# One MLP's second product as seven block products instead of eight, with operands that pass through DRAM

## The chip, the core and the metric

The kernel runs on one core of a Trainium2 chip. The core has five engines, each with its own queue of instructions that it works through in order: TensorE (PE) multiplies matrices and writes to PSUM, VectorE (DVE) and ScalarE (ACT) do elementwise work, GpSimd (POOL) does elementwise work on SBUF alone, and SyncE (SP) issues the DMA transfers between DRAM and SBUF. The engines meet at semaphores. The metric is the time of one execution on the device in microseconds (us); the number given for a kernel is the median of several runs.

## The reference, cut to what matters

The reference is one inference step of a decoder with two layers, for a prompt of 1024 positions and 32 sample positions (1056 columns in all). Layer 0 mixes dilated attention and causal pooling, layer 1 is an mLSTM block, and after each of them stands a squared-ReLU MLP with a residual:

```
def sq_relu_ffn(x, w1, w2):
    h = jax.nn.relu(x @ w1)
    return (h * h) @ w2
...
        hp = hp + sq_relu_ffn(rms_norm(hp, norm_ffn[layer]), ffn_w1[layer], ffn_w2[layer])
```

with x of width 1024, w1 of 1024x4096 and w2 of 4096x1024. The change is in the MLP of layer 0 alone.

## The kernel before, in words

Activations lie transposed: 128 channels on the partitions, the 1056 positions along the free dimension. A product is made to high precision from three passes. Each operand is split into a rounded part and a rest (`split`, L97: the rounded part by ACT at L106, the rest by a DVE or POOL subtraction at L107), and `mm3` (L129) multiplies rounded by rounded, rounded by rest and rest by rounded into one PSUM bank. The columns come in three pieces, `CH`: 384, 384 and 288.

`ffn` (L236) works through the 4096 hidden channels in eight blocks of 512. For a block it makes four rows of 128 hidden channels (first product: eight k tiles, three passes, three column pieces, so 72 matmuls a row). DVE takes a finished bank out with relu and the norm's factor (L254), ACT squares it (L255) and rounds it (L106), DVE makes the rest (L107). Then `project_into` (L262) multiplies the block by its part of w2 (second product: eight output rows of 128, four k tiles, three passes, three pieces) and DVE adds each bank to the residual `x` (L274). The weights of a row or a pair of rows are one DMA of 512 KB into `wraw` and a split by ACT and POOL.

In the last block every finished piece of `x` is also fed onward (`feed`, L181): two DVE instructions scale it by the next norm's gain and split it into the operands `xg` of the next layer (L187 and L188), ACT squares it (L199), POOL sums the squares (L201), and `finish_norm` turns the sum into the factor `R`. The next layer's first product, `project(0)` in `up_project`, reads `xg`, and its banks are multiplied by `R`.

A framework schedules the program: it keeps the order of each engine's queue by priorities and its own estimates, gives out buffers as they come free, and sets the semaphore waits. A pool that is opened where another was closed takes its memory, and waits for that memory's last readers and writers. In the MLP of layer 0 there are four PSUM banks (`self.psum(4)`).

Of the kernel before, what the change touches and what calls it, by code (L numbers as in the profile page):

```python
# [22 lines left out]
CH = [(0, 384), (384, 384), (768, 288)]  # L23
FF = 4096
FB = 512
EPS = 1e-6

H, HD = 8, 64
# [15 lines left out]
def weave(*steps, beat=lambda: None):  # L44

    order = sorted(((k + 0.5) / n, i) for i, (_, n) in enumerate(steps) for k in range(n))
    for _, i in order:
        next(steps[i][0], None)
        beat()


def late(n, gen):

    for _ in range(n):
        yield
    yield from gen
# [11 lines left out]
class Net:  # L68
# [4 lines left out]
    def __init__(self, tc, a):  # L73
        self.tc, self.nc, self.a = tc, tc.nc, a
        nc = self.nc
        self.cms = []
        self.consts = self.pool("consts")
        self.wpool = self.pool("wpool", bufs=2)
        self.gains = self.consts.tile([P, 5, KD], F32, name="gains")
        self.ident = self.consts.tile([P, P], F32, name="ident")  # L80
        self.ones = self.consts.tile([P, P], F32, name="ones")
        nc.gpsimd.memset(self.ones, 1.0)
        self.mhalf = self.consts.tile([P, 16], F32, name="mhalf")
        nc.gpsimd.memset(self.mhalf, -0.5)
# [3 lines left out]
        self.due, self.parts = [], {}  # L88
        self.beside, self.pace = None, 0

    def pool(self, name, bufs=1, side="left", **kw):
# [34 lines left out]
            self.split(w[0][:, k], w[1][:, k], raw[:, k], eng=eng)  # L126
        return w

    def mm3(self, ps, w, x, first=True, last=True):  # L129

        mm = self.nc.tensor.matmul
        mm(ps, w[0], x[0], start=first, stop=False)  # L132
        mm(ps, w[0], x[1], start=False, stop=False)  # L133
        mm(ps, w[1], x[0], start=False, stop=last)  # L134

    def psum(self, bufs):
        self.pmm, self.tag, self.bufs = self.pool("pmm", space=PSUM), "mm", bufs
# [97 lines left out]
    def ffn(self, layer, x, xg, fed, beside=None):  # L235

        nc = self.nc
# [20 lines left out]
        if layer:  # L258
            self.settle()
        self.close(hp)  # L260

    def project_into(self, x, unit, xs, fed=None, first=None, pool=None):  # L262

# [464 lines left out]
    def up_project(self, keep):  # L728
# [23 lines left out]
        def project(m):  # L752
# [84 lines left out]
        rest = (None for m in range(16) for _ in outer(m))  # L837
        left = 15
        for m in range(16):
            weave((project(m), 13), *([(late(3, follow(*self.made)), 11)] if m else []))  # L840
# [741 lines left out]
```

## Time and profile before

| | |
|---|---|
| median of 3 runs | 3201.49 us (3197.26 to 3202.69) |
| the profiled execution | 3198.09 us, span of its trace 3196.3 us |
| PE busy | 3100.5 us, 97% of the span, 19702 matmuls |
| DVE busy | 1675.6 us, 52% |
| ACT busy | 995.4 us, 31% |
| POOL busy | 923.2 us, 29% |
| the MLP of layer 0 | from 548 us to 1300 us of the span |
| granted TensorE clock, mean | 0.992 of full speed |

Times in the trace count from the start of the span. Busy time of PE is the time in which at least one matmul is under way; matmuls are pipelined, so the time that one matmul adds is read from the distance between two starts, not from its own duration. A wait is put down to the semaphore that came last.

### The profile page before, as it was taken

The numbers are of one execution on the slowest core, as the hardware profiler recorded it, in microseconds if no ns is written. First come the engines' busy times: TensorE is split into PE (matmuls) and PEld (weight loads), VectorE is DVE, ScalarE is ACT, GpSimd is POOL, SyncE is SP. The second block draws the span as 40 slices with busy tenths as digits, with TensorE's granted clock in tenths as the row PEclk, the third lists the DMA queues.
The fourth block names the chain that finished last, engine by engine and source line by source line (L and its number), as shares of the span: only waits on it lengthen the run. The fifth ranks groups of instructions, "written<-read, shape, count | busy, mean of one in ns | idle before, by whom it ended". The sixth has DMA issues, their size and how long they took to land.

```text
span 3196.3 us, 48197 instructions
## 1 busy us (share of the span) xinstructions
PE 3100.5 (97%) x19702; PEld 2888.7 (90%) x19702; DVE 1675.6 (52%) x3139; ACT 995.4 (31%) x1828; POOL 923.2 (29%) x691
## 2 busy tenths in 40 slices
PE   7999999999999999999998999998999999999998
PEld 7775578999999999999998888878999999999998
DVE  7765537333333335666565477766365444444434
ACT  4443212222211123222223565654123222222222
POOL 4110014221122223434333354543142212121223
PEclk9999999999999999999999999999999999999999
DMA  4113561111111111333323466555314444444411
GB/s 134 45 47 131 179 228 40 42 45 47 47 47 47 47 47 67 103 107 110 102 94 122 146 207 222 179 165 179 107 40 137 150 159 165 148 155 142 146 60 68
DMA packets 198790, 355.85 MB, mean 111 GB/s; under 512 B 25540, under 2 KB 103108, under 8 KB 195752
## 3 DMA queue, kind: packets, MB, share of 16 engines
q1 hardware_dynamic: 198568, 352.77, 32.7%
q8 instruction: 154, 2.52, 0.3%
q14 instruction: 68, 0.56, 0.1%
HBM read 263.61 MB, written 89.11 MB: 110 GB/s over the span
## 4 chain that ended last, share of the span: by engine, by line
PE 81%; DVE 10%; POOL 2%; ACT 2%; issue 2%; DMA 2%; SPq 0%; DVEq 0%; POOLq 0%; ACTq 0%
PE mm L132 23%; PE mm L134 22%; PE mm L133 22%; PE po L406 1%; PE nq L132 1%; PE mm L534 1%; DVE xg L188 1%; PE nq L134 1%; PE nq L133 1%; PE pt L390 1%; PE pc L1320 1%; DVE x L274 1%; DVE xg L187 1%; PE acc L1263 1%; POOL xm L107 1%
## 5 line engine op out<-in xcount | busy, mean ns | idle before, releaser
L107 POOL TENSOR_TENSOR w<-wraw,w 128x1024 fp32r<-128x1024 f32 x196 | 478.2, 2440 | 1524.9 <-ACT w L106 1513.5
L132 PE MATMUL mm<-xg,w 128*128 128x384 f32 (+1 forms) x2664 | 886.6, 333 | 15.0 <-ACT xg L458 6.7
L134 PE MATMUL mm<-xg,w 128*128 128x384 f32 (+1 forms) x2664 | 866.0, 325 | 7.6 <-POOL w L107 7.6
L133 PE MATMUL mm<-xg,w 128*128 128x384 f32 (+1 forms) x2664 | 866.2, 325 | 4.3 <-DVE xg L459 4.3
L132 PEld LDWEIGHTS mm<-xg,w 128*128 128x128 f32 x2664 | 504.3, 189 | 59.6 <-issue 43.9
L274 DVE TENSOR_TENSOR x<-mm,x 128x384 f32<-128x384 f32 (+1 forms) x528 | 275.3, 523 | 531.4 <-PE mm L134 523.0
L133 PEld LDWEIGHTS mm<-xg,w 128*128 128x128 f32 x2664 | 505.0, 190 | 13.0 <-DVE xg L459 5.8
L134 PEld LDWEIGHTS mm<-xg,w 128*128 128x128 f32 x2664 | 503.8, 189 | 12.2 <-POOL w L107 9.2
L132 PE MATMUL mm<-h,w 128*128 128x384 f32 (+1 forms) x1536 | 497.5, 324 | 0.0
L134 PE MATMUL mm<-h,w 128*128 128x384 f32 (+1 forms) x1536 | 497.1, 324 | 0.0
L133 PE MATMUL mm<-h,w 128*128 128x384 f32 (+1 forms) x1536 | 495.9, 323 | 0.0
L106 ACT ACTIVATE w<-wraw 128x1024 fp32r<-128x1024 f32 (+1 forms) x202 | 210.7, 1046 | 807.5 <-PE mm L133 643.5
L107 DVE TENSOR_TENSOR h<-hr,h 128x384 fp32r<-128x384 f32 (+1 forms) x192 | 198.8, 1035 | 213.6 <-ACT h L106 213.6
L133 PEld LDWEIGHTS mm<-h,w 128*128 128x128 f32 x1536 | 289.1, 188 | 3.6
L134 PEld LDWEIGHTS mm<-h,w 128*128 128x128 f32 x1536 | 288.8, 188 | 0.0
L132 PEld LDWEIGHTS mm<-h,w 128*128 128x128 f32 x1536 | 288.7, 188 | 0.0
L254 DVE SCALAR_TENSOR_TENSOR hr<-mm,rstd 128x384 f32<-128x384 f32 (+1 forms) x192 | 100.6, 524 | 259.5 <-PE mm L134 259.4
L255 ACT ACTIVATE hr<-hr 128x384 f32<-128x384 f32 (+1 forms) x192 | 94.6, 493 | 382.8 <-DVE hr L254 382.7
L779 DVE SCALAR_TENSOR_TENSOR ca<-ext,chan,ca 128x1080 f32<-128x1080 f32 x48 | 132.8, 2766 | 1.5
L132 PE MATMUL mm<-yh,w 128*128 128x384 f32 (+1 forms) x384 | 126.0, 328 | 6.0 <-ACT yh L106 6.0
L133 PE MATMUL mm<-yh,w 128*128 128x384 f32 (+1 forms) x384 | 125.8, 328 | 0.4 <-DVE yh L107 0.4
L134 PE MATMUL mm<-yh,w 128*128 128x384 f32 (+1 forms) x384 | 125.6, 327 | 0.0
(366 smaller groups left out, 4838.4 us busy)
## 6 DMA issues: line engine op xcount, KB each, us to landing
wraw<-in_ffn_w SPq DMA_DIRECT2D x128, 512.0 KB, 3.2
c<-in_state_C SPq DMA_DIRECT2D x32, 1024.0 KB, 5.8
c<-in_state_C SPq DMA_DIRECT2D x64, 512.0 KB, 3.8
out_o_sC<-c SPq DMA_DIRECT2D x64, 512.0 KB, 3.0
wraw<-in_ml_w_in SPq DMA_DIRECT2D x32, 512.0 KB, 3.5
kc<-in_cache_k SPq DMA_DIRECT2D x32, 448.0 KB, 4.0
vc<-in_cache_v SPq DMA_DIRECT2D x14, 1024.0 KB, 6.3
wraw<-in_ab_w_in SPq DMA_DIRECT2D x16, 512.0 KB, 3.5
```

Source lines behind the costliest of these rows:

```text
L106: nc.scalar.activation(hi, src, AF.Copy)
L107: (eng or nc.vector).tensor_tensor(lo, src, hi.bitcast(F32), op=OP.subtract)
L132: mm(ps, w[0], x[0], start=first, stop=False)
L133: mm(ps, w[0], x[1], start=False, stop=False)
L134: mm(ps, w[1], x[0], start=False, stop=last)
L187: nc.vector.tensor_scalar(hi, src, gain, None, op0=OP.mult)
L188: nc.vector.scalar_tensor_tensor(lo, src, gain, hi.bitcast(F32), op0=OP.mult, op1=OP.subtract)
L254: nc.vector.scalar_tensor_tensor(r, ps, 0.0, self.R[:, c0:c0 + cw], op0=OP.max, op1=OP.mult)
L255: nc.scalar.activation(r, r, AF.Square)
L274: self.nc.vector.tensor_tensor(xm, ps, xm, op=OP.add)
L390: nc.tensor.transpose(pt[:, j * P:(j + 1) * P], prs[j][:, kt * P:(kt + 1) * P], self.ident)
L779: nc.vector.scalar_tensor_tensor(ca[:, :o], ext[:, j:j + o], k[:, j:j + 1], ca[:, :o], op0=OP.mult, op1=OP.add)
```

## The change

The MLP of layer 0 goes through a new function, `ffn7`, in two stages that no longer alternate; the MLP of layer 1 stays as it was. Strassen's scheme in Winograd's form splits the second product into 2x2 blocks: over output rows (two of 128), over k (two halves) and over positions (two halves of 528, `HT`). Seven products of block sums take the place of eight block products.

The first stage, `up_parts`, makes all 4096 hidden channels. After every two rows of 128, DVE forms the four sums of position halves that the scheme needs (L278 to L280), ACT and DVE split the seven operands into rounded part and rest (L108, L109), in two column halves of 264 (`CS`), and each half goes to a DRAM tensor `hd` (L284, 128 x 7 x 528 numbers, 1.89 MB). The second stage, `down`, loads the seven operands of a block of 512 channels into tiles `T0` to `T6` (L337, 128 x 2112 numbers, 1.08 MB each). Each has one buffer, and its pool takes the memory that the first stage's pool has left. A unit is a block and a pair of output rows: `down_weights` loads the weights, forms four sums on DVE (L318 to L321, 128x256 each) and splits seven operands in four pieces on ACT and POOL (three of 128x512, one of 128x256). PE makes seven products for each of two column halves, and DVE adds or subtracts the accumulated bank into `x` after each of them (L358, 128x264). There are 28 such units over seven blocks, and for the last block eight units of one column half each, so that the first half's columns are finished early; these make the weights' sums and splits twice, and feed the next layer in pieces of 264. In the next layer, `project(0)` takes its columns in four pieces of 264.

The core of the diff:

```
+    ORDER = (0, 2, 5, 3, 4, 1, 6)
...
+        def operands(kb, j, hs):
+            tt = nc.vector.tensor_tensor
+            tt(hs[:, 4:6], hs[:, 1:3], hs[:, 0:1].to_broadcast([P, 2, HT]), op=OP.subtract)
+            tt(hs[:, 6], hs[:, 2], hs[:, 4], op=OP.add)
+            tt(hs[:, 7], hs[:, 3], hs[:, 6], op=OP.subtract)
+            for c in range(2):
+                st = hp.tile([P, 7, 2, CS], F32R, name="st", tag="st", bufs=2)
+                self.split(st[:, :, 0], st[:, :, 1], hs[:, 1:, c * CS:(c + 1) * CS])
+                nc.sync.dma_start(hd[kb, :, :, c, j].rearrange("i p l t -> p i l t"), st.bitcast(F32))
...
+        def load(kb, i):
+            T[i] = sp.tile([P, 2, 2, 2, CS], F32R, name=f"T{i}", tag=f"T{i}")
+            nc.sync.dma_start(T[i].bitcast(F32), hd[kb, i])
...
+        runs = [(kb, mp, (0, 1)) for kb in range(nb - 1) for mp in range(4)]
+        runs += [(nb - 1, mp, (c,)) for c in range(2) for mp in range(4)]
...
+                    for c in cs:
+                        n1, n2 = HT + c * CS, c * CS
+                        if i in (0, 2, 3):
+                            {0: B, 2: D, 3: E}[i][c] = self.bank(CS)
+                        ps = (D if i == 2 else E if i in (3, 1) else B)[c]
+                        for k in range(2):
+                            self.mm3(ps, [w[k][:, 0], w[k][:, 1]], [T[i][:, c, k, l] for l in range(2)],
+                                     k == 0 and i in (0, 2, 3), k == 1, more=True)
...
+                        elif i == 1:
+                            add(m, n2, ps, OP.subtract)
+                            if fed and kb == nb - 1:
+                                fed(m, n2, CS)
+                                fed(m + 1, n2, CS)
...
+                    if kb < nb - 1 and mp == 3:
+                        load(kb + 1, i)
...
+    def ffn7(self, layer, x, xg, fed):
+        hd = self.dram.tile([FF // FB, 7, P, 2, 2, 2, CS], F32, name="hd")
+        hp = self.pool("up", side="right")
+        self.up_parts(layer, xg, hp, hd)
+        self.close(hp)
+        self.down(layer, x, hd, fed)
...
-            for c0, cw in CH:
+            for c0, cw in CH if m else [(0, CS), (HT, CS), (CS, CS), (HT + CS, CS)]:
...
-        self.ffn(0, self.x, self.xg, lambda m, c0, cw: self.feed(self.x[:, m, c0:c0 + cw], self.xg, 2, m, c0, cw))
+        self.ffn7(0, self.x, self.xg, lambda m, c0, cw: self.feed(self.x[:, m, c0:c0 + cw], self.xg, 2, m, c0, cw))
```

Three places show how the queues now stand. The first is SP's queue where the first stage ends and the second begins (`st` are the operands on their way out, `T` on their way in, `wraw` the weights); before, this queue held nothing but weights here:

```order
L119 DMA wraw_5280<-in_ffn_w1 128x1024
L119 DMA wraw_5378<-in_ffn_w2 128x1024
L119 DMA wraw_5468<-in_ffn_w2 128x1024
L119 DMA wraw_5558<-in_ffn_w2 128x1024
L119 DMA wraw_5648<-in_ffn_w2 128x1024
```

```order
L303 DMA wraw_7969<-in_ffn_w2 128x1024
L284 DMA hd_4959<-st_7769 128x7x528
L284 DMA hd_4959<-st_7773 128x7x528
L284 DMA hd_4959<-st_7955 128x7x528
L284 DMA hd_4959<-st_7959 128x7x528
L337 DMA T0_7971<-hd_4959 128x2112
L337 DMA T2_7973<-hd_4959 128x2112
L337 DMA T5_7975<-hd_4959 128x2112
L337 DMA T3_7977<-hd_4959 128x2112
L337 DMA T4_7979<-hd_4959 128x2112
L337 DMA T1_7981<-hd_4959 128x2112
L337 DMA T6_7983<-hd_4959 128x2112
```

The first load of the second stage stands behind the last two stores of the first, and waits for both to land, since its memory was theirs. The second place is PE's queue in the first unit of block 1, where the tile `T6` is used (the bank `mm_8510` belongs to that unit, `mm_8633` to the next one):

```order
L136 MATMUL mm_8641<-T5_8426,w_8580 128x264
L134 MATMUL mm_8633<-T4_8468,w_8611 128x264
L135 MATMUL mm_8633<-T4_8468,w_8611 128x264
L136 MATMUL mm_8633<-T4_8468,w_8611 128x264
L134 MATMUL mm_8510<-T6_8505,w_8507 128x264
L135 MATMUL mm_8510<-T6_8505,w_8507 128x264
L136 MATMUL mm_8510<-T6_8505,w_8507 128x264
```

The scheduler has put 27 matmuls of the next unit (products 0, 5 and half of 4) ahead of the product with `T6`, the tile that is loaded last; the other six are used in the order in which they are loaded. The third place is DVE's queue in the last block, where the next layer is fed. Before, a piece had one addition and two feeding instructions:

```order
L274 TENSOR_TENSOR x<-mm,x 128x384
L187 TENSOR_SCALAR xg_88<-x,gains 128x384
L188 SCALAR_TENSOR_TENSOR xg_89<-x,gains,xg_88 128x384
L274 TENSOR_TENSOR x<-mm,x 128x288
L187 TENSOR_SCALAR xg_88<-x,gains 128x288
L188 SCALAR_TENSOR_TENSOR xg_89<-x,gains,xg_88 128x288
```

```order
L189 TENSOR_SCALAR xg_88<-x,gains 128x264
L358 TENSOR_TENSOR x<-x,mm 128x264
L190 SCALAR_TENSOR_TENSOR xg_89<-x,gains,xg_88 128x264
L358 TENSOR_TENSOR x<-x,mm 128x264
L318 TENSOR_TENSOR s<-wraw 128x256
L320 TENSOR_TENSOR s<-wraw 128x256
L319 TENSOR_TENSOR s<-s,wraw 128x256
L358 TENSOR_TENSOR x<-x,mm 128x264
L321 TENSOR_TENSOR s<-s,wraw 128x256
L358 TENSOR_TENSOR x<-x,mm 128x264
```

Now additions of shorter pieces, the same two feeding instructions and the weights' four sums stand between each other.

## Rows read from the trace of the kernel before

**Rows 1.** Busy by stretch: us, PE PEld DVE ACT POOL (instructions), clock, DMA share, GB/s.

```profile
1250.00:1310.00 60.00, 56.83 (x351) 56.08 (x349) 48.07 (x83) 16.42 (x31) 31.74 (x29) 0.97 0.30 106
560.00:1240.00 680.00, 680.00 (x4224) 679.94 (x4222) 229.57 (x353) 152.97 (x246) 145.06 (x61) 1.00 0.14 47
```

**Rows 2.** Groups by form, 560 to 1350 us: count | busy us, mean ns | idle before.

```profile
L132 PE MATMUL mm<-h,w 128*128 128x384 f32 x512 | 172.9, 338 | 0.0
L132 PE MATMUL mm<-h,w 128*128 128x288 f32 x256 | 75.7, 296 | 0.0
```

**Rows 3.** PE's instructions in order of time: start us, duration us, what.

```profile
1025.71 0.29 PE L132 MATMUL mm<-xg,w 128*128 128x288 f32 x1
...
1028.90 0.34 PE L132 MATMUL mm<-xg,w 128*128 128x384 f32 x1
...
1033.12 0.34 PE L132 MATMUL mm<-xg,w 128*128 128x384 f32 x1
...
1902.63 0.28 PE L132 MATMUL x<-ch,wp 128*128 128x256 f32 x1
...
1904.66 0.28 PE L134 MATMUL x<-ch,wp 128*128 128x256 f32 x1
```

**Rows 4.** Groups by form of DVE, ACT and POOL, 560 to 1350 us.

```profile
L107 POOL TENSOR_TENSOR w<-wraw,w 128x1024 fp32r<-128x1024 f32 x66 | 159.4, 2415 | 547.6 <-ACT w L106 547.3 <-ACT gw L726 0.2
L274 DVE TENSOR_TENSOR x<-mm,x 128x384 f32<-128x384 f32 x128 | 71.1, 557 | 160.0 <-PE mm L134 159.8
L106 ACT ACTIVATE w<-wraw 128x1024 fp32r<-128x1024 f32 x66 | 69.9, 1060 | 343.3 <-PE mm L133 335.4 <-issue 5.3 <-DMA wraw<-in_ffn_w 2.6
L274 DVE TENSOR_TENSOR x<-mm,x 128x288 f32<-128x288 f32 x64 | 29.3, 457 | 58.2 <-PE mm L134 58.2
L201 POOL TENSOR_TENSOR ss<-ss,sq 128x384 f32<-128x384 f32 x14 | 17.0, 1217 | 14.3 <-ACT sq L199 14.3
L254 DVE SCALAR_TENSOR_TENSOR hr<-mm,rstd 128x288 f32<-128x288 f32 x32 | 14.6, 458 | 29.1 <-PE mm L134 29.1
L255 ACT ACTIVATE hr<-hr 128x288 f32<-128x288 f32 x32 | 13.7, 428 | 0.0
L201 POOL TENSOR_TENSOR ss<-ss,sq 128x288 f32<-128x288 f32 x5 | 4.4, 871 | 3.9 <-ACT sq L199 3.9
L782 DVE TENSOR_TENSOR ca<-ca,sg 128x1080 f32<-128x1080 f32 x2 | 2.6, 1283 | 1.6 <-ACT sg L781 1.6
```

**Rows 5.** Instructions of L107, L187, L188, 552 to 1310 us: ns min/median/max.

```profile
L107 DVE TENSOR_TENSOR h<-hr,h x96: 552/559/2450, 558.0 to 1251.5; 128x384 fp32r<-128x384 f32 x64, 128x288 fp32r<-128x288 f32 x32
...
L187 DVE TENSOR_SCALAR xg<-x,gains x24: 357/421/2941, 1254.0 to 1302.4; 128x384 fp32r<-128x384 f32 x16, 128x288 fp32r<-128x288 f32 x8
...
L188 DVE SCALAR_TENSOR_TENSOR xg<-x,gains,xg x24: 503/618/1470, 1254.4 to 1305.4; 128x384 fp32r<-128x384 f32 x16, 128x288 fp32r<-128x288 f32 x8
```

**Rows 6.** DVE's and POOL's instructions in order of time, around 1299 us.

```profile
1299.27 1.75 DVE L187 TENSOR_SCALAR xg<-x,gains 128x288 fp32r<-128x288 f32 x1
...
1298.20 2.66 POOL L107 TENSOR_TENSOR w<-wraw,w 128x1024 fp32r<-128x1024 f32 x1 [0.51 <-ACT w L106]
```

**Rows 7.** Busy by stretch: loads of `x`, then stores to DRAM.

```profile
448.00:464.00 16.00, 14.71 (x91) 14.39 (x90) 4.99 (x10) 1.06 (x1) 2.40 (x1) 1.00 1.01 418
1304.00:1306.00 2.00, 2.00 (x8) 2.00 (x8) 1.85 (x2) 0.00 (x0) 1.16 (x1) 0.50 1.07 379
```

**Rows 8.** DMA issues: count, KB each, median us from issue to landing.

```profile
wraw<-in_ffn_w SPq DMA_DIRECT2D x128, 512.0 KB, 3.2
...
x<-in_x SPq DMA_DIRECT2D x4, 1056.0 KB, 9.1
```

**Rows 9.** PE at the end of the MLP, and the stretch behind it.

```profile
1302.50 0.41 PE L132 MATMUL mm<-xg,w 128*128 128x384 f32 x1 [2.17 <-DVE x L274]
...
1303.00:1306.00 3.00, 3.00 (x13) 3.00 (x12) 2.85 (x2) 0.00 (x0) 2.16 (x1) 0.59 1.02 360
```

More of the change, by code (lines that the diff above doesn't have):

```diff
@@ L127, in wparts, with mm3 @@
         return w
-    def mm3(self, ps, w, x, first=True, last=True):
+    def mm3(self, ps, w, x, first=True, last=True, more=False):
         mm = self.nc.tensor.matmul
-        mm(ps, w[0], x[0], start=first, stop=False)
-        mm(ps, w[0], x[1], start=False, stop=False)
-        mm(ps, w[1], x[0], start=False, stop=last)
+        mm(ps, w[0], x[0], start=first, stop=False, skip_group_check=more)
+        mm(ps, w[0], x[1], start=False, stop=False, skip_group_check=more)
+        mm(ps, w[1], x[0], start=False, stop=last, skip_group_check=more)
     def psum(self, bufs):
@@ L260, in ffn, with up_parts @@
         self.close(hp)
+    ORDER = (0, 2, 5, 3, 4, 1, 6)
+    def up_parts(self, layer, xg, hp, hd):
+        nc = self.nc
+        def operands(kb, j, hs):
[7 more added lines that the diff above has]
+                nc.sync.dma_start(hd[kb, :, :, c, j].rearrange("i p l t -> p i l t"), st.bitcast(F32))
+        for m in range(FF // P):
+            w = self.wunit(self.a["ffn_w1"][layer, m])
+            if m % 2 == 0:
+                hs = hp.tile([P, 8, HT], F32, name="hs", tag="hs", bufs=2)
+            row = hs[:, m % 2 * 2:m % 2 * 2 + 2].rearrange("p b t -> p (b t)")
+            for c0, cw in CH:
+                ps = self.product(self.tiles(w), self.tiles(xg), c0, cw)
+                h = row[:, c0:c0 + cw]
+                nc.vector.scalar_tensor_tensor(h, ps, 0.0, self.R[:, c0:c0 + cw], op0=OP.max, op1=OP.mult)
+                nc.scalar.activation(h, h, AF.Square)
+            if m % 2:
+                operands(m // 4, m // 2 % 2, hs)
@@ new lines, in down, with prepare @@
+    def down(self, layer, x, hd, fed):
+        nc = self.nc
+        sp = self.pool("down", side="right")
+        nb = FF // FB
+        T = {}
+        def load(kb, i):
[3 more added lines that the diff above has]
+        runs += [(nb - 1, mp, (c,)) for c in range(2) for mp in range(4)]
+        units = [self.down_weights(self.a["ffn_w2"][layer, kb, mp], sp) for kb, mp, _ in runs]
+        slots = [(u, s) for u in range(len(runs)) for s in range(4)]
+        ready = {}
+        def prepare(n):
+            if n < len(slots):
+                u, s = slots[n]
+                ready[n] = next(units[u])
+                if s == 2 and u + 2 < len(runs):
+                    next(units[u + 2])
+        for u in range(2):
+            next(units[u])
+        for i in self.ORDER:
+            load(0, i)
+        for n in range(3):
+            prepare(n)
+        add = lambda m, t, ps, op=OP.add: nc.vector.tensor_tensor(x[:, m, t:t + CS], x[:, m, t:t + CS], ps, op=op)
+        for u, (kb, mp, cs) in enumerate(runs):
+            m = 2 * mp
+            B, D, E = {}, {}, {}
+            order = iter(self.ORDER)
+            for s in range(4):
+                n = 4 * u + s
+                prepare(n + 3)
+                for w in ready.pop(n):
+                    i = next(order)
+                    for c in cs:
[6 more added lines that the diff above has]
+                                     k == 0 and i in (0, 2, 3), k == 1, more=True)
+                        self.tick()
+                        if i == 0:
+                            add(m, n1, ps)
+                        elif i == 2:
+                            add(m, n1, ps)
+                            if fed and kb == nb - 1:
+                                fed(m, n1, CS)
+                        elif i == 5:
+                            add(m, n2, ps)
+                        elif i == 3:
+                            add(m + 1, n2, ps, OP.subtract)
+                        elif i == 4:
+                            add(m + 1, n2, ps)
+                        elif i == 1:
+                            add(m, n2, ps, OP.subtract)
+                            if fed and kb == nb - 1:
+                                fed(m, n2, CS)
+                                fed(m + 1, n2, CS)
+                        else:
+                            add(m + 1, n1, ps)
+                            if fed and kb == nb - 1:
+                                fed(m + 1, n1, CS)
+                    if kb < nb - 1 and mp == 3:
+                        load(kb + 1, i)
+        self.close(sp)
```

29 lines of the change are left out of this document (28 added, 1 removed).

## The prediction

> **What bounds the kernel now.** I read the busy times by stretch first. In the MLP of layer 0 PE has no idle time at all from 560 to 1240 us: 4224 matmuls in 680 us, 0.161 us each, at full clock, while DVE is busy for a third of it and POOL for a fifth [rows 1]. The reader is to see that a matmul taken away there is time gained, and that DVE and POOL have room beside it. The last stretch, 1250 to 1310 us, where the next layer is fed, is another picture: DVE is busy 48.1 of 60 us, POOL 31.7, PE loses 3.2 us [rows 1]. Then I read the distances between matmuls and the cost of each operation by its form [rows 2 to 5], and the DMA rates [rows 7, 8], since the change hangs work between PE's two products that the trace of before does not have.
>
> **The gain.** The second product has 768 matmuls for each of three lines, 2304 in all [rows 2]. From start to start a piece of 384 takes (1033.12 - 1028.90) / 24 = 0.1758 us and one of 288 takes (1028.90 - 1025.71) / 24 = 0.1329 us; with a width of 256 seventeen steps take 2.03 us, 0.1194 us each [rows 3]. Before: 2304 x 0.161 = 370.9 us. After: 28 units of 7 products x 2 column halves x 6 = 84 matmuls and eight units of 42, 2688 matmuls of 264 columns. Between 256 and 288 lies 0.1228 us for 264, so 330.1 us. The gain is 40.8 us, not an eighth of 370.9 us (46.4), since narrower matmuls cost a little more per column.
>
> **The first stage.** PE's part is unchanged: two rows of hidden channels are 144 matmuls, 23.2 us. A DVE instruction with both sources in SBUF takes 0.15 us and 1.05 ns a column, from 552 ns at 384 columns and 1283 ns at 1080 [rows 4, 5]. Per two rows DVE does six bank passes (3.1 us), sums of 1056, 528 and 528 columns (2.7 us) and two rests of 1848 (4.2 us): 10 us of 23.2. ACT has six squares of about 0.5, two roundings of 1.8 and two of weights of 1.06: 9 us. The stores, 3.8 MB, take 10 us at the 379 GB/s of the stretch with stores [rows 7]. All of it lies beside PE, whose four banks cover some 15 us of a late DVE; cost 0. Were that cover gone, each us by which DVE's group of sums overran it would cost 16 us, once per pair of rows. The next layer's first row takes four pieces of 264 in place of three: 96 x 0.1228 = 11.8 us for 11.6, 0.2 us, left out; the four weight loads that the last block makes twice find the DMA engines busy for 0.30 of that stretch [rows 1].
>
> **Between the stages.** After the first stage's last matmul PE has nothing to do until the first operand is back. The chain: bank pass 0.46, square 0.43 [rows 4], last sum of 528 columns 0.70, ACT's rounding of 1848 columns 1.77 (from 428 ns at 288 and 1060 ns at 1024 [rows 4]), DVE's rest 2.1, five handovers of about 0.05: the first store is issued at 5.7 us, the second one rest later. A store is 1.89 MB, 5.0 us at 379 GB/s. From issue to landing 512 KB take 3.2 us [rows 8], of which 1.25 us are its bytes at 418 GB/s [rows 7]; so 1.95 us are fixed. Both stores have landed at 5.7 + 1.95 + 10 = 17.6 us. Only then the first load is issued, and lands at 17.6 + 1.95 + 2.6 = 22.1 us; the others follow at 2.6 us each (1.08 MB at 418 GB/s), the sixth at 35 us. PE has by then only five products of 12 matmuls (1.47 us each) to do, so it loses 35 - 7.4 = 27.6 us; the seventh product is covered, because 27 matmuls of the next unit stand before it in the queue. After a wait of 2.17 us the clock stood at 0.59 over 3 us and 13 matmuls ran where 17 had room [rows 9], 1.3 us lost; I add that. Together 29 us, from 25 (a store at 418 GB/s, shorter handovers) to 34 (DVE held by POOL twice for 2.4 us).
>
> **From block to block.** Each operand tile has one buffer, so block k+1's operand i is loaded when the last unit of block k has used it. Products end every 1.47 us, loads land every 2.6 us: the sixth lands at 1.47 + 1.95 + 6 x 2.6 = 19.0 us after that unit's start and is wanted at 10.3 + 5 x 1.47 = 17.7 us. 1.3 us, seven times: 9 us. Bounds: 0, and 20 us if the loads run at the stores' 379 GB/s. What waits behind it is the whole of PE's queue.
>
> The Trainium skill, "DMA: Bandwidth & Descriptors", section Specifications, puts one core's share of DRAM at about 358 GB/s. By that a load would be 3.0 us, the two terms 32 and 26 us, and the sum 20 us worse. The trace shows 418 GB/s over 16 us [rows 7], and the measurement decides.
>
> **Inside a unit.** DVE has 14 additions of 264 columns (457 ns at 288, 557 at 384 [rows 4], so 0.432 us) and four sums of 256 (0.42 us): 7.7 us of PE's 10.3. An addition must be done before its bank is written again three groups of six matmuls later, 2.2 us. Sums that stand between additions can use that up at times; no row shows this, so 0 to 14 us over 28 units (up to half a us each), and I take 4, near the nothing that PE loses to DVE in rows 1.
>
> **The last block.** Here a unit has one column half: 42 matmuls, 5.16 us of PE. DVE has 7 additions (3.0 us), four pairs of feeding instructions (0.34 and 0.47 us at 264, from the minima and medians 357 and 421, 503 and 618 ns [rows 5]; 3.3 us) and four sums (1.7 us): 8.0 us. Eight units: PE 41 us, DVE 64. POOL has three splits of 512 (about 1.5 us by 2415 ns at 1024 and 1217 at 384), one of 256 (1.0) and four sums of squares (0.8, from 1217 and 871 ns [rows 4]): 8.6 us a unit, 69 in all. So PE is no longer the bound. And DVE waits for POOL: a feeding instruction that takes 0.36 us took 1.75 us and ended when POOL's split did [rows 6]. In the old last block DVE's 48.1 us [rows 1] hold at most 12 us of such waits: 24 additions 12.6 us and 48 feeding instructions at their shortest 23.5 us leave 12.0, 0.25 us per feeding instruction. Now 96 instructions are exposed, so 0 to 24 us; I take half, 12 us, and with 2 us for the norm's small instructions 78 us. Less PE's 41 and 3 us of DVE's work that lies behind PE's last matmul: 34 us. Bounds: 20 (no waits) and 64 (POOL's 69 us and DVE's exposed 40 us never together). The old block's own 3.2 us I leave, since the norm's chain behind the last product is the same.
>
> **The sum.** -40.8 + 29 + 9 + 4 + 34 = +35 us against the profiled execution's 3198.1 us: 3233 us. The median of the runs is 3.4 us above that execution, so 3237 us.
>
> **Rivals.** *The port.* That one wait of rows 6 may be the rule: DVE's exposed instructions and POOL's never run together. Then the last block takes 109 us, the term is 65 instead of 34, and the time 3267 us. The Trainium skill, "SBUF — State Buffer", section "Who interferes with whom", has this as a rule: VectorE with two SBUF inputs or in a two-port mode and GpSimd lock each other out for a whole instruction. Rows 6 agree, but by that rule alone the count of collisions is open. Against it: POOL's work often follows DVE's, and the old block's waits were at most 0.25 us.
>
> *Faster.* PE stays the bound in the last block, because the scheduler has mixed its units so that DVE's sums and feeding fall where PE is busy with others. Then only the gap between the stages and the block changes remain: -40.8 + 29 + 2 + 5 = -5, and with a store path shorter by some us, -12: 3190 us. It decides if DVE and POOL need under 47 us for the last block. Against it stand 64 us of DVE without any wait.
>
> *The clock.* In the last block PE works half of the time, in short pieces, and the granted clock may fall to 1.2 GHz as it did behind a wait [rows 9]. Its 41 us become 82, as much as DVE's 78, and as the two wait for each other I put it at 95: +17, 3254 us.
>
> *The additions hold PE up in every unit*: half a us and the block changes at their high end, +21: 3258 us.
>
> **How the numbers follow.** My sum 0.48, the port 0.14, the clock 0.1, the additions 0.1, the faster rival 0.18. About 0.2% (6.4 us) is what a measurement of this kernel can tell from no change: of my sum 0.04, its low end, falls within that, and of the faster rival 0.05, its -5. So faster 0.13, same 0.09, slower 0.78. My sum with each term at its low end is -40.8 + 25 + 0 + 0 + 20 = +4, 3205 us; the range goes down to the faster rival's -5, 3197 us, and leaves out what is below. High: the last block at 64 and the additions at 14, the rest at my values: -40.8 + 29 + 9 + 14 + 64 = +75, 3277 us.
>
> **What would show it.** Right: PE idle for about 28 us once, with stores and then loads in the DMA rows; seven short stops at the first unit of a block, on loads; PE half busy over some 80 us before the next layer, waiting for DVE. Wrong: matmuls of 264 columns well off 0.123 us; a first stage in which PE stops; a last block in which PE runs through. The gap between the stages decides most: if it were under 15 us, the change would come near to even.

## The result and the profile after

The changed kernel takes 3275.27 us, median of 4 runs (3269.94 to 3281.61), beside 3201.6 us for the kernel before on the same chip: ratio 1.0233, 95% interval 1.0213 to 1.0254. It is 74 us slower, where 35 were forecast. The profiled execution took 3274.4 us, its span 3272.6, so 76.3 us more span than before.

Where they lie, from the starts of PE's matmuls: the MLP of layer 0 grew from 752.2 to 818.5 us (+66.3), all that follows by 10.7, and what precedes it lost 0.7. The stretches of the changed kernel (us from:to, length, busy time and count of PE, PEld, DVE, ACT, POOL, clock, DMA share, GB/s), in answer to [rows 1]:

```profile
560.00:900.00 340.00, 340.00 (x2113) 339.94 (x2112) 166.88 (x160) 118.50 (x146) 69.60 (x29) 1.00 0.57 202
924.00:946.40 22.40, 0.20 (x2) 0.00 (x0) 9.82 (x13) 5.28 (x6) 3.19 (x3) 0.57 0.63 234
993.40:1274.80 281.40, 260.05 (x2020) 252.23 (x2019) 181.41 (x433) 55.71 (x96) 115.47 (x97) 0.99 0.52 208
1274.80:1365.80 91.00, 65.49 (x362) 60.27 (x360) 77.98 (x149) 28.36 (x63) 58.18 (x57) 0.77 0.27 102
1366.00:1400.00 34.00, 28.49 (x178) 27.89 (x177) 12.13 (x24) 7.31 (x14) 13.60 (x20) 0.80 0.62 213
```

In order: the first product, where PE never stops; the gap, where PE stands still; blocks 1 to 6 of the second product; its last block; the next layer's first row. PE's matmuls of 264 columns start 0.122 us apart (1.46 us for twelve steps), in answer to [rows 3], and the gap ends with a load:

```profile
946.43 0.56 PE L134 MATMUL mm<-T,w 128*128 128x264 f32 x1 [22.23 <-DMA T<-hd]
...
1015.21 0.28 PE L135 MATMUL mm<-T,w 128*128 128x264 f32 x1
...
1016.67 0.28 PE L135 MATMUL mm<-T,w 128*128 128x264 f32 x1
```

So 2688 x 0.122 = 327.9 us of matmuls stand for 370.9: -43.0. To that come the gap of 22.4 us and 6.0 more in the first block's two first units, 28.4; blocks 1 to 6, whose 2016 matmuls are 246.0 us of 281.4: 35.4; the last block, 336 matmuls or 41.0 us of 91.0: 50.0. Less the 3.2 us that the old last block lost [rows 1] this is +67.6, against 66.3 measured.

Block 1's start, beside [rows 8] and [rows 9]: PE's waits in order of time, then the stretch around the second, then the loads issued from 984 to 1006.2 us (KB each, median us from issue to landing):

```profile
998.70 0.36 PE L134 MATMUL mm<-T,w 128*128 128x264 f32 x1 [0.62 <-DMA T<-hd]
1002.45 0.56 PE L134 MATMUL mm<-T,w 128*128 128x264 f32 x1 [2.05 <-DMA T<-hd]
```

```profile
1000.00:1002.00 2.00, 0.39 (x4) 0.18 (x2) 0.56 (x2) 0.63 (x1) 0.81 (x1) 1.00 1.01 414
1002.00:1004.00 2.00, 1.55 (x7) 1.58 (x8) 0.00 (x0) 0.00 (x0) 0.45 (x1) 0.61 0.99 407
1004.00:1006.00 2.00, 2.00 (x12) 2.00 (x12) 0.86 (x2) 0.00 (x0) 0.00 (x0) 0.54 1.03 434
```

```profile
T<-hd SPq DMA_DIRECT2D x7, 1056.0 KB, 11.5
wraw<-in_ffn_w SPq DMA_DIRECT2D x2, 512.0 KB, 11.1
```

The reader is to see that the loads run at 407 to 434 GB/s, about the 418 of [rows 7], that PE waits for them (here for the fourth and the fifth operand) and that its granted clock stands at 0.61 and 0.54 of full speed behind the wait: 10 matmuls begin in the last 2 us where 16 had room.

Taken from the starts of PE's matmuls, each step less 0.122 us, the 35.4 us of blocks 1 to 6 are 17.4 at 16 waits for operand loads, 6.4 at 8 waits for DVE's additions, 1.0 at a wait for ACT, 9.4 in 84 slow steps, as I call those of more than 0.18 us with no wait before them (most are 0.22 us), and 1.1 in all the others.

The last block by form (count | busy us, mean ns | idle before), beside [rows 4] and [rows 5], and some of DVE's and POOL's instructions in order of time, beside [rows 6]:

```profile
L190 DVE SCALAR_TENSOR_TENSOR xg<-x,gains,xg 128x264 fp32r<-128x264 f32 x30 | 25.1, 850 | 0.1
L358 DVE TENSOR_TENSOR x<-x,mm 128x264 f32<-128x264 f32 x56 | 23.1, 420 | 8.5 <-PE mm L136 8.5
L189 DVE TENSOR_SCALAR xg<-x,gains 128x264 fp32r<-128x264 f32 x31 | 22.7, 745 | 0.2
L203 POOL TENSOR_TENSOR ss<-ss,sq 128x264 f32<-128x264 f32 x24 | 19.7, 826 | 3.2 <-ACT ss L197 2.0 <-ACT sq L201 0.7
```

```profile
1277.66 1.27 POOL L109 TENSOR_TENSOR w<-wraw,w 128x512 fp32r<-128x512 f32 x1 [1.41 <-ACT w L108]
...
1277.77 1.45 DVE L190 SCALAR_TENSOR_TENSOR xg<-x,gains,xg 128x264 fp32r<-128x264 f32 x1
...
1284.00 0.43 DVE L358 TENSOR_TENSOR x<-x,mm 128x264 f32<-128x264 f32 x1 [0.89 <-PE mm L136]
1285.32 0.43 DVE L358 TENSOR_TENSOR x<-x,mm 128x264 f32<-128x264 f32 x1 [0.89 <-PE mm L136]
1285.78 0.36 DVE L189 TENSOR_SCALAR xg<-x,gains 128x264 fp32r<-128x264 f32 x1
...
1289.80 0.49 DVE L190 SCALAR_TENSOR_TENSOR xg<-x,gains,xg 128x264 fp32r<-128x264 f32 x1
```

A feeding instruction that begins while POOL's split runs ends 0.29 us after the split (1277.77 + 1.45 and 1277.66 + 1.27); alone it takes 0.36 or 0.49 us. Taken over the block, 85 instructions of DVE work on SBUF alone: 61 feeding instructions and 24 of the weights' sums. Of the 48 that began while a POOL instruction ran, 45 were lengthened; of the 37 that began while POOL was idle, one was, though POOL began during 11 of the others. All 46 lengthened ones ended 0.15 to 0.16 us (L189) or 0.28 to 0.29 us (the others) after a POOL instruction. The additions, which read PSUM, take 0.42 us either way. And DVE waits too: two additions stand 1.32 us apart, since PE's six matmuls take 1.32 us there in place of 0.73, at 0.22 us each.

PE's waits in the last block (us in total, times, longest):

```profile
PE mm L134 <- DVE x L358: 11.8, 9, 2.9
PE mm L136 <- POOL w L109: 4.5, 3, 2.7
PE mm L222 <- POOL ss L203: 4.1, 2, 3.7
PE mm L134 <- DMA T<-hd: 3.0, 3, 1.6
```

So PE stood at DVE's additions, and also at POOL itself: at the splits of weights and at the sums of squares. The waits for operands are the seventh block change. Slow steps are 170 here and lose 18.5 us.

### The profile page after: what moved, and what is told of

Read it like the earlier page. It is cut to its first block, busy times and chain, and to the rows that moved or that the text cites. A ratio compares the mean times of both kernels' runs of the same rounds, so it can differ in the third digit from the quotient of the medians.

```text
span 3272.6 us, 50124 instructions
## 1 busy us (share of the span) xinstructions
PE 3107.1 (95%) x20122; PEld 2882.6 (88%) x20122; DVE 1869.9 (57%) x3544; ACT 1049.8 (32%) x1885; POOL 1014.5 (31%) x811
## 4 chain that ended last, share of the span: by engine, by line
PE 75%; DVE 11%; DMA 6%; issue 3%; POOL 2%; ACT 2%; SPq 0%; DVEq 0%; POOLq 0%; ACTq 0%
PE mm L134 20%; PE mm L136 19%; PE mm L135 19%; DMA T<-hd 3%; PE nq L134 2%; DVE xg L190 2%; PE po L553 1%; PE nq L136 1%; PE nq L135 1%; PE mm L681 1%; POOL w L109 1%; DVE xg L189 1%; PE pt L537 1%; PE pc L1467 1%; PE acc L1410 1%
## 5 line engine op out<-in xcount | busy, mean ns | idle before, releaser
L134 PE MATMUL mm<-xg,w 128*128 128x384 f32 (+2 forms) x2672 | 890.3, 333 | 13.3 <-ACT xg L605 6.6
L109 POOL TENSOR_TENSOR w<-wraw,w 128x1024 fp32r<-128x1024 f32 (+1 forms) x236 | 475.6, 2016 | 1353.1 <-ACT w L108 1342.3
L136 PE MATMUL mm<-xg,w 128*128 128x384 f32 (+2 forms) x2672 | 869.2, 325 | 7.6 <-POOL w L109 7.6
L135 PE MATMUL mm<-xg,w 128*128 128x384 f32 (+2 forms) x2672 | 869.5, 325 | 4.3 <-DVE xg L606 4.3
L108 ACT ACTIVATE w<-wraw 128x1024 fp32r<-128x1024 f32 (+2 forms) x242 | 214.5, 888 | 634.8 <-PE mm L135 354.3
L421 DVE TENSOR_TENSOR x<-mm,x 128x384 f32<-128x384 f32 (+1 forms) x336 | 174.8, 522 | 313.4 <-PE mm L136 305.0
L134 PE MATMUL mm<-T,w 128*128 128x264 f32 x896 | 271.7, 304 | 63.0 <-DMA T<-hd 42.5
L136 PE MATMUL mm<-T,w 128*128 128x264 f32 x896 | 263.0, 295 | 4.6 <-POOL w L109 4.5
L135 PE MATMUL mm<-T,w 128*128 128x264 f32 x896 | 262.6, 293 | 0.0
L134 PE MATMUL mm<-h,w 128*128 128x384 f32 (+1 forms) x768 | 249.0, 324 | 0.0
L358 DVE TENSOR_TENSOR x<-x,mm 128x264 f32<-128x264 f32 x448 | 185.3, 424 | 111.4 <-PE mm L136 109.4
L136 PE MATMUL mm<-h,w 128*128 128x384 f32 (+1 forms) x768 | 248.7, 324 | 0.0
L135 PE MATMUL mm<-h,w 128*128 128x384 f32 (+1 forms) x768 | 247.9, 323 | 0.0
L134 PEld LDWEIGHTS mm<-T,w 128*128 128x128 f32 x896 | 177.3, 198 | 75.6 <-DVE x L358 25.5
L136 PEld LDWEIGHTS mm<-T,w 128*128 128x128 f32 x896 | 176.5, 197 | 5.5 <-POOL w L109 5.4
L135 PEld LDWEIGHTS mm<-T,w 128*128 128x128 f32 x896 | 178.0, 199 | 0.0
L109 DVE TENSOR_TENSOR h<-hr,h 128x384 fp32r<-128x384 f32 (+1 forms) x96 | 99.2, 1034 | 93.5 <-ACT h L108 93.5
L135 PEld LDWEIGHTS mm<-h,w 128*128 128x128 f32 x768 | 144.8, 188 | 3.6
L109 POOL TENSOR_TENSOR w<-s,w 128x512 fp32r<-128x512 f32 x72 | 97.9, 1362 | 159.0 <-ACT w L108 159.0
```

What stands on the lines that cost most here:

```text
L108: nc.scalar.activation(hi, src, AF.Copy)
L109: (eng or nc.vector).tensor_tensor(lo, src, hi.bitcast(F32), op=OP.subtract)
L134: mm(ps, w[0], x[0], start=first, stop=False, skip_group_check=more)
L135: mm(ps, w[0], x[1], start=False, stop=False, skip_group_check=more)
L136: mm(ps, w[1], x[0], start=False, stop=last, skip_group_check=more)
L358: add = lambda m, t, ps, op=OP.add: nc.vector.tensor_tensor(x[:, m, t:t + CS], x[:, m, t:t + CS], ps, op=op)
```

## The experiments

Each of the first seven is compared with the changed kernel's 3275 us; all were timed beside the kernel before, whose median was 3198.6 to 3199.8 us in those sessions and 3201.6 in the changed kernel's. So 2 to 3 us of a difference between two times can be the session's; the ratios to the kernel before, in brackets, are free of it, and smaller effects are read from the stretches of the traces.

**Last block whole.**

```
-runs = [(kb, mp, (0, 1)) for kb in range(nb - 1) for mp in range(4)]
-runs += [(nb - 1, mp, (c,)) for c in range(2) for mp in range(4)]
+runs = [(kb, mp, (0, 1)) for kb in range(nb) for mp in range(4)]
```

> The last block's four units run whole (both column halves), as in the blocks before, not in eight half units: its weights are split and summed once, not twice. In the changed kernel the last block takes 91 us where PE has 41 us of work; DVE is busy about 77 of it, POOL 57, and the 61 feeding instructions take 24 us more than their 0.34 and 0.47 us. Theory (DVE is the bound and waits for POOL on the feeding instructions): 16 sums fewer are about 9 us of DVE, half of POOL's weight splits gone takes about half of the 24 us of waits: the block falls to about 70 us, the time from 3275 to about 3254. Rival (only DVE's own count matters, no port): 9 us less, 3266. Rival (PE at half clock bounds it): the block stays within 5 us, 3270 to 3278.

Measured 3252.76 us (1.017, 1.0155 to 1.0185). With this order the next layer's first row reads the norm of some columns before it is written, so only the last block is compared:

```profile
1273.50:1340.20 66.70, 49.40 (x344) 45.99 (x342) 61.63 (x123) 19.52 (x44) 37.53 (x39) 0.92 0.31 121
```

66.7 us, DVE 61.6, POOL 37.5, the clock 0.92. Under the rival's 82, and somewhat under the theory's 70. PE works in longer runs here, and its clock is 0.92 where it was 0.77, so the run does not tell DVE's part from PE's.

**First feeding instruction on ACT.**

```
-nc.vector.tensor_scalar(hi, src, gain, None, op0=OP.mult)
+nc.scalar.activation(hi, src, AF.Copy, scale=gain)
```

> The first of the two feeding instructions of the last block (gain times x, 32 pieces of 264 columns) is done by ACT in place of DVE. It took 0.85 us each on DVE, 25 us in all. Theory (DVE with its waits for POOL is the bound of the last block): DVE loses 15 us of its own work and half of the exposed instructions, ACT has room (32 x 0.43 = 14 us more): the block falls from 91 to about 68 us, 3252. Rival (POOL's 57 us and the handovers from engine to engine set the block): less than 6 us, 3269 to 3276. Rival (PE's half clock): 3270 to 3276.

Measured 3260.41 us (1.0191, 1.0175 to 1.0206):

```profile
1274.10:1353.90 79.80, 59.53 (x362) 53.34 (x360) 66.32 (x118) 39.85 (x92) 58.28 (x57) 0.87 0.30 115
```

Half of the theory's gain. The instruction that was moved had 22.7 us of DVE (0.745 us each; the 0.85 and 25 us of the expectation belong to the second one, L190). DVE loses 11.7 us of busy time, because the sums of the weights, 0.45 to 0.68 us by their means in the changed kernel, now take 0.63 to 1.24; the waits for POOL move to other instructions. DVE's 13 us of idle time stay.

**POOL's sums of squares left out.**

```
-if m < KD - 2 or c0 + w < NT:
+if w == CS and m < KD - 2:
+    pass
+elif m < KD - 2 or c0 + w < NT:
     nc.gpsimd.tensor_tensor(ss, ss, sq, op=OP.add)
```

> POOL's 24 sums of squares in the last block (20 of its 60 us there) are left out, so the norm of the next layer is wrong; DVE's own instructions stay the same. In the changed kernel a feeding instruction of DVE takes 0.35 and 0.49 us where POOL is idle and 0.84 and 0.89 us where POOL works, about 25 us of waits in the last block. Theory (these are waits for POOL, and they set the block): a third of POOL's work less takes some 6 to 10 us of the waits, the block goes from 91 to 81 to 85 us, the time to about 3267. Rival (DVE's own count and the handovers set the block, the long durations are only where DVE had nothing to do): within 2 us, 3273 to 3277.

Measured 3267.54 us (1.0218, 1.0202 to 1.0233). The last block, then its feeding instructions by form:

```profile
1279.00:1365.80 86.80, 61.08 (x362) 56.55 (x360) 72.17 (x148) 27.94 (x62) 42.14 (x37) 0.82 0.28 107
```

```profile
L190 DVE SCALAR_TENSOR_TENSOR xg<-x,gains,xg 128x264 fp32r<-128x264 f32 x30 | 23.5, 796 | 0.1
L189 DVE TENSOR_SCALAR xg<-x,gains 128x264 fp32r<-128x264 f32 x30 | 19.7, 670 | 0.2
```

Not one instruction of DVE was changed, and DVE is busy 5.8 us less, the block 4.2 us shorter. So the waits for POOL are real time of DVE, and in this pair of traces the block shortened by most of what DVE did (one feeding instruction fewer lies in this stretch, some 0.7 us). The size is under the 6 to 10 us expected, and the ratios of the two kernels to the one before (1.0218 and 1.0233) agree within their intervals.

**Eight banks.**

```
-self.psum(4)
+self.psum(8)
```

> Eight PSUM banks in place of four for this MLP, nothing else. PE may then run more groups ahead of DVE's additions. Theory (DVE has too much to do in the last block; a longer reach doesn't give it time; block changes wait for loads): the last block stays at 85 to 91 us, the block changes as they are, 3269 to 3276. Rival (the short reach of four banks makes PE stop at every late addition, in the last block and in the first units of each block): the last block falls by 15 us or more and the units after a block change by 1 us each, 3240 to 3255.

Measured 3244.01 us (1.014, 1.0123 to 1.0157). Blocks 1 to 6 and the last block:

```profile
991.20:1249.70 258.50, 249.81 (x2018) 246.94 (x2017) 179.80 (x432) 55.71 (x96) 113.72 (x97) 1.00 0.56 226
1249.70:1341.20 91.50, 63.97 (x362) 58.17 (x360) 78.66 (x149) 28.92 (x63) 57.70 (x57) 0.81 0.27 101
```

My theory held for the last block (91.5 us) and fell for the block changes: 258.5 us where 246 are matmuls, so 12.5 lost in place of 35.4. The loads land as late as before, but the order is another. Of the changed kernel and then of this one, PE's matmuls of block 1 in the order of its queue, from the fourth product on; 8389, 8407, 8426, 8444, 8468, 8484, 8505 are products 0, 2, 5, 3, 4, 1, 6:

```
four banks:  8444 x12, 8468 x12, 8484 x12, 8389 x12, 8426 x12, 8468 x3, 8505 x12
eight banks: 8444 x12, 8389 x12, 8407 x3, 8468 x12, 8407 x9, 8426 x6, 8484 x12, 8426 x6
```

With eight banks there is room to begin the next unit's products 0 and 2 ahead of 4, and 2 and 5 ahead of 1: their operands are there, while the loads of 4 and 1 are under way. (With four banks the next unit's product 4 stands ahead of 6 with 3 of its 12 matmuls, not with half.) So the loads bound the block change, and the four banks decided that PE had nothing to put in.

**Fewer weight loads at the block changes.** The edit in short:

```
-raw = self.wpool.tile(...); nc.sync.dma_start(raw, ...)
+if not kept:                       # kept: units 1 and 2 of blocks 1 to 6
+    self.raw = self.wpool.tile(...); nc.sync.dma_start(self.raw, ...)
+raw = self.raw
```

> In blocks 1 to 6 the second and third unit use the raw weights of the first (12 weight loads of 512 KB left out, the ones that are issued while the next block's operands are loaded; the splits stay). So the second product is computed with wrong weights there; only the time is meant. Theory (the two weight loads stand between the operand loads in the same DMA queues: 1.05 MB at 418 GB/s is 2.5 us, and the wait they cause drops the clock): each of the six block changes falls from about 5.9 us to about 2.5, some 20 us in all, 3255; PE's wait on the sixth and on the earlier loads shrinks. Rival (DVE's additions, late after the block change, set the loss): under 5 us, 3270 to 3276. Rival (the queue alone, without the clock): about 12 us, 3263.

Measured 3268.05 us (1.0217, 1.02 to 1.0234):

```profile
992.30:1270.40 278.10, 257.25 (x2019) 249.47 (x2018) 175.53 (x432) 55.63 (x96) 111.36 (x97) 1.00 0.46 187
```

3.3 us less than the 281.4 of the changed kernel: the theory's size fell. The edit tells less than it was meant to. In its trace one weight load is still issued just ahead of each block's first operand, since the raw buffer comes free at the same place; only the load ahead of the seventh operand is gone. DVE's waits at its sums moved rather than went: 13.2 us for loads and 0.9 for POOL in the changed kernel, 4.7 and 14.9 here.

**Half of each operand load.** The edit in short:

```
-dma_start(T[i], hd[kb, i])
+dma_start(T[i][:, :, 0], hd[kb, i, :, :, 0])    # and the matmuls read k = 0 twice
```

> Of each operand only the first half (one of its two rows of channels) is loaded, and used twice, so the second product is wrong; 0.54 MB a load in place of 1.08, PE, DVE and POOL do the same work. Theory (the pace of the operand loads, 2.57 us each against 1.47 us of PE per product, sets the first unit of each block and the gap): the six block changes fall from 5.9 to about 1.2 us each (28 us), the first block's 5.7 us goes, and the gap of 22.4 us before the first product falls by about 1.3: the time goes from 3275 to about 3241. Rival (DVE's late additions hold PE up at the block changes): less than 10 us, 3266 to 3275.

Measured 3243.62 us (1.0143, 1.0126 to 1.0159). Blocks 1 to 6, and the waits in them (us in total, times, longest):

```profile
988.60:1249.40 260.80, 251.14 (x2018) 248.57 (x2017) 178.16 (x432) 55.64 (x96) 113.18 (x97) 0.99 0.39 137
```

```profile
DVE s L318 <- DMA wraw<-in_ffn_w: 24.6, 24, 2.6
PEld mm L134 <- DVE x L358: 11.9, 11, 2.5
PE mm L134 <- DVE x L358: 9.5, 8, 2.3
```

The same stretch in the changed kernel:

```profile
PEld mm L134 <- DVE x L358: 16.5, 23, 2.5
PE mm L134 <- DMA T<-hd: 14.7, 16, 2.1
PE mm L134 <- DVE x L358: 5.1, 8, 2.3
DVE s L318 <- DMA wraw<-in_ffn_w: 13.2, 17, 2.6
```

PE's waits on operands are gone, and with them 20.6 of the 35.4 us: the load pace is shown. PE's remaining waits are for DVE's additions, and they grew from 5.1 to 9.5 us, while DVE stands 24.6 us at sums of the weights until their loads land. So by the waits the rest has a cause in the same queue: PE's banks wait for additions that stand behind such a sum. No run took these weight loads away beside the halved operands.

**Stores of x by halves.** The stream goes to DRAM behind the MLP.

```
-for c0, cw in CH:
-    nc.sync.dma_start(xd[:, :, c0:c0 + cw], self.x[:, :, c0:c0 + cw])
+for c0 in (0, HT, CS, HT + CS):
+    nc.sync.dma_start(xd[:, :, c0:c0 + CS], self.x[:, :, c0:c0 + CS])
```

> The changed kernel with one edit behind the MLP: the stream x goes to DRAM in four pieces of 264 columns, in the order in which the last block finishes them, not in pieces of 384, 384 and 288, which all have columns of both halves. In the changed kernel the three stores (4.2 MB) are all issued at 1365 to 1366.6 us, and DVE's convolution of the next layer waits until 1393.8 for a small load behind them (6.8 us on POOL's copy of it), where it waited for nothing before. Theory (the pile of stores delays that load): two of the four stores go 40 us earlier, the wait falls by 4 to 6 us: 3275 to about 3270. Rival (the first row's extra 7.4 us come from PE's half clock there and the four pieces): within 1.5 us, 3274 to 3276.

Measured 3266.31 us (1.0215, 1.0201 to 1.0229). DVE's last scaling of the first row and its convolution, first of the changed kernel, then of this one:

```profile
1386.83 0.18 DVE L912 TENSOR_TENSOR ext<-mm,rstd 128x32 f32<-128x32 f32 x1
1393.78 0.84 DVE L924 TENSOR_SCALAR ca<-ext,chan 128x1080 f32<-128x1080 f32 x1 [6.77 <-POOL ext L904]
```

```profile
1385.49 0.18 DVE L912 TENSOR_TENSOR ext<-mm,rstd 128x32 f32<-128x32 f32 x1
1385.77 0.84 DVE L924 TENSOR_SCALAR ca<-ext,chan 128x1080 f32<-128x1080 f32 x1
```

The wait of 6.8 us is gone. From PE's last matmul of the MLP to its first `pv` matmul, which in the changed kernel waits 4.9 us for an instruction of DVE behind this convolution, the kernel before takes 23.4 us, the changed kernel 30.6 and this one 23.5: of 7.3 us lost, 0.1 are left.

**Three edits together**, the first row's pieces in the order of their columns.

> Three edits together: the last block whole, the first feeding instruction on ACT, eight banks; the next layer's first row takes its four pieces in the order of their columns. Alone they gave -22, -15 and -31 us against the changed kernel. Theory (they act in different places: the last block for the first two, block changes for the third): the last block goes to about 56 us (DVE 24 + 16 + 7 + waits of about 10), the block changes stay at 2 us: 3275 - 31 - 35 = about 3209. Rival (in the last block PE then waits for something else, POOL or the additions, and the two gains overlap): 3220 to 3228.

Measured 3215.4 us (1.0056, 1.0041 to 1.0071):

```profile
992.40:1252.00 259.60, 250.23 (x2018) 247.09 (x2017) 179.18 (x432) 55.66 (x96) 113.99 (x97) 1.00 0.56 225
1252.00:1302.20 50.20, 44.66 (x338) 43.09 (x336) 44.97 (x89) 28.31 (x68) 36.81 (x36) 0.97 0.35 142
```

The last block is 6 us better than expected and the rest 12 worse. The next layer's first matmul comes 9.0 us after the MLP's last one, with the norm's work between them (1.0 us in the changed kernel), and up to its first `pv` matmul the next layer loses 15.8 us against the kernel before.

**Units in pairs,** on the three edits. The change of the loops in short:

```
-for s: for w in the slot's products:            one unit
+for s: for j in the slot's products: for d in range(2):   unit u + d
```

> As the kernel with three edits, and the units go in pairs: each product is done for two units before the next, so an operand is used for 2.94 us and the next one lands every 2.57. Theory (load pace): the block changes cost nothing, and the first block's five late loads are covered too, the gap of 22.4 us stays: the second product loses 22 + 0 to 5 us before the last block; the time is 8 to 15 us under that of the kernel with three edits, about 3197. Rival (the weights of two units at once, with one pair of raw buffers, come late behind the operand loads: 1.05 MB behind up to 7 loads): a stop of 3 to 6 us per pair of units, 3215 to 3260.

Measured 3197.72 us (0.9995, 0.9985 to 1.0004):

```profile
987.90:1236.50 248.60, 247.44 (x2019) 246.59 (x2017) 197.40 (x433) 54.31 (x95) 112.10 (x96) 1.00 0.62 235
```

Blocks 1 to 6 lose 2.6 us. With the three edits alone they lost 13.6 (259.6 less 246.0) and in the changed kernel 35.4, so the pairs are worth 11.0 us of it, and the rest came with the eight banks. No difference from the kernel before can be measured.

**Stores by rows of tiles, on the pairs.** `xd[:, m:m + 2]` for each m, in place of columns.

> As the kernel with pairs; x goes to DRAM in four pieces of two rows of tiles, each when its units are done, so half of the 4.2 MB go some 25 us earlier. Theory (the stores' pile at the end delays the loads of the next layer): the 8.5 us that the next layer's first row loses there fall to 4 or 5: 3197.7 to about 3194. Rival (the loss there is the norm's chain and the last feeding): no change, 3196 to 3199.

Measured 3198.79 us (1.0, 0.9991 to 1.0009). A miss, and the rival's time: earlier stores changed nothing. The next layer's first matmul comes 7.4 us after the MLP's last one (6.9 with pairs alone), with the norm's work between them.

**Two operands early, on that.** Operands 0 and 2 have memory of their own, and each block a DRAM tensor of its own; the sums' buffer is single.

> As the kernel with pairs and stores by rows; the first two operands of the first block have memory of their own and are loaded during the first product (the buffer for the sums is single there, to make room). Theory (the gap is the chain from the last rows' stores to the third operand's load, and PE now has 48 matmuls, 5.9 us, to do in it): the gap of 22.6 us shrinks to 16 to 17 in all, 3194 to about 3188, under the kernel before by 0.3%. Rival (with a single buffer for the sums DVE's chain of 7 us after each pair of rows holds up the bank passes, and PE stops in the first product 16 times): slower by up to 30 us, 3195 to 3225.

Measured 3194.28 us (0.9989, 0.998 to 0.9998). PE goes straight on into 48 matmuls, and the wait that follows is

```profile
945.51 0.56 PE L134 MATMUL mm<-T,w 128*128 128x264 f32 x1 [16.47 <-DMA T<-hd]
```

16.5 us in place of 22.3 with pairs. The rival's stops did not come: PE is busy 340.00 us from 560 to 900. The median is 4 us under the kernel before, where 10 were expected; the interval leaves out 1, but the difference is less than the 0.2% that the prediction took as the bound, so it does not pass for a gain.

**The kernel before with eight banks.** The same edit as above.

> The kernel before, with eight PSUM banks in this MLP and nothing else: it tells whether the eight banks alone are worth something without the block products. Theory (the kernel before has no waits of PE between 560 and 1240 us, and loses 3.2 us in its last block): 3196 to 3200, no difference that can be measured. Rival (its last block and the next layer's first row wait for banks): 3190 to 3195, and then the best kernel with block products gains nothing over it.

Measured 3199.09 us (0.9998, 0.9989 to 1.0007): no difference can be measured, so the banks alone are worth nothing here without the block products.

## Why the prediction was right or wrong

- *The gain, -40.8.* Right: -43.0, since a matmul of 264 columns adds 0.122 us, not 0.1228.
- *The first stage, 0.* Right: PE is busy 340.00 of 340 us.
- *Between the stages, +29.* Right: 28.4. The order of the chain held too: with two operands in hand the wait was 16.5 us.
- *From block to block, +9, and inside a unit, +4.* Together 13; measured 35.4 over blocks 1 to 6, that is over six of the seven changes. This is the term that failed most. The step was "the sixth lands at 1.47 + 1.95 + 6 x 2.6 = 19.0 us after that unit's start". By the completion records of block 1 it landed at 21.6 us, and the fourth and fifth, on which PE stood (0.62 and 2.05 us), at 15.3 and 19.1 where the same sum gives 13.8 and 16.4. Three things were not in the sum. A weight load of 512 KB (1.25 us) is issued just ahead of the first operand; I had the weight loads in my table of work and not in this queue. The first operand's issue comes 0.5 us later for it. And from the fifth load on, the last of a load's sixteen parts landed 1.2 us behind the other fifteen. The trace has a packet there that the DMA table calls `instruction` (queue q8, 16 KB): it began at 999.7 us and took 1.1 us. With eight banks such a packet began at 992.9 us, took 1.0, and the last parts were 1.1 to 1.2 us late from the load that landed at 994.9; in block 4 one began at 1137.1 us, took 1.1, and the last parts were 1.3 us late from the load that landed at 1141.3; in the first block's seven loads, 941 to 962 us, there is no such packet, and the last part came within 0.02 us of the one before. So the lateness goes with these packets; that they cause it no run shows. Then come two things that the step left out: the granted clock of 0.54 to 0.61 behind the wait (9.4 us in slow steps over the six blocks), and DVE, which stood up to 2.6 us at a sum until its weights had landed, with PE's additions behind it. The load pace is shown (halving it gave back 20.6 us). DVE's stop as the rest is read from the waits, not from an edit, and the weight loads' own share is not shown, since that run left one of the two.
- *The last block, +34.* 50. DVE's busy time came out as forecast, 78.0 us, but for reasons that cancelled: the feeding instructions' waits for POOL are 23 us by their means, (745 - 349) x 31 + (850 - 488) x 30 ns, not 12; against that neighbouring instructions of DVE overlap, so that 87.6 us of durations are 78.0 us of busy time. That this number came out is luck. What failed is that DVE runs through the block. It was idle for 13 us, 8.5 of them waiting for PE, which ran at 0.77 of its clock; and the 3 us that I took off for DVE's work behind PE's last matmul were not there: 34 + 13 + 3 = 50. Told from PE's side, by the starts of its matmuls, the 50 us are 13.2 at waits for DVE's additions, 9.5 at waits for POOL (weight splits and sums of squares), which my path from PE to DVE did not have, 5.9 for loads and ACT, 18.5 in slow steps and 2.9 for the norm's 24 small matmuls. So the block is neither DVE's alone nor PE's: each waits for the other, POOL holds both up, and PE's slow steps delay DVE's additions. What the clock alone is worth here no run shows.
- *The port.* As a mechanism it is shown: POOL's work taken away shortened DVE's unchanged instructions, and every lengthened one ended behind a POOL instruction. The Trainium skill, "SBUF — State Buffer", section "Who interferes with whom", has the lock; the trace agrees for the feeding instructions and shows that the additions, which read PSUM, took 0.42 us either way. What fell is "never run together": POOL was busy for 58.2 us (69 priced), DVE's exposed instructions need 35.4 undisturbed (40 priced), and the two together were busy for 73.9 us, not 93.6. Of 12 DVE instructions during which POOL began, having been idle, 11 kept their time. That the block's 91 us lie near those 93.6 is chance, since PE's waits and slow steps are part of them.
- *The clock*, priced at 95 us for the block: in part. It stood at 0.77 of full speed, not at 1.2 GHz throughout, and PE was busy for 65.5 us, not 82; the block was 91.
- *The additions in every unit*, and *faster*: neither. Over the 24 units of blocks 1 to 6 PE waited 8 times for an addition, 5.1 us in all; and DVE needed 78 us and POOL 58 in the last block, not under 47.
- *Behind the MLP, nothing.* 10.7 us were lost. 7.3 are shown, since stores in the order of the halves took them back: the last block ends in halves of 264 columns, so all three stores of x (4.2 MB) are issued at the end, and a small load behind them held DVE. The prediction did not follow the change past its own last instruction. The other 3.4 us differ between kernels and stay open.

## What to carry to other kernels

A saving in matmuls has to be set against the pace at which its operands come: where a buffer is refilled while it is last used, list every transfer in that queue in order, the small ones too, and compare the landing times with the times of use. Reusing each operand for two units in a row (2.94 us of use against 2.57 of load) took the loss over six blocks from 13.6 to 2.6 us. And follow a change to the first wait of the next stage, since the order in which a block's columns are finished decides when everything behind it may start.

## What the runs showed that I had not expected

- PSUM banks worked as a scheduling window: with four more banks ready matmuls go ahead of waiting ones, and blocks 1 to 6 take 22.9 us less, of 31 in the whole time; in the kernel before they gave nothing.
- Whether a DVE instruction on SBUF pays for POOL is settled by who begins first: of 48 that began while POOL worked 45 were lengthened, of 37 that began while it was idle one was.
- A DVE instruction freed of POOL moves the collision to the next: with the feeding on ACT, the sums of the weights took 0.63 to 1.24 us each where they had taken 0.45 to 0.68.
- Two DVE instructions in a row overlap: the last block's 87.6 us of durations are 78.0 us of busy time.
- One 16 KB packet of the queue that the DMA table calls `instruction`, 1.0 to 1.1 us long, goes with a last part that is 1.1 to 1.3 us late in every operand load that lands behind it in the same row of loads (blocks 1 and 4, and block 1 with eight banks).
